# Routing of the second half of the tokens one head behind the first, two buffers of gates, gathers issued later

## The chip, the cores and the metric

The kernel runs on one core of a Trainium2 chip. The metric is the time of one execution on the device in microseconds (us), as the median of three runs. Engines: TensorE (PE) multiplies matrices, VectorE (DVE), ScalarE (ACT) and GpSimd (POOL) compute elementwise, and SyncE (SP) issues transfers between memory and the on-chip buffer. GpSimd issues the indirect transfers (gathers). Each engine takes its instructions strictly in the order in which they are written down for it.

## The reference

One layer of a decoder: two groups of attention heads, their output projection, and then PEER, a layer of 16,384 experts of one neuron each. The change is about PEER:

```
q = (xt @ w_query).reshape(T, PEER_HEADS, 2, PEER_HALF)
scores = jnp.einsum('thpc,hpnc->thpn', q, sub_keys)
vals, idx = lax.top_k(scores, PEER_TOPK)
cand = (vals[..., 0, :, None] + vals[..., 1, None, :]).reshape(T, PEER_HEADS, 256)
top_vals, top_c = lax.top_k(cand, PEER_TOPK)
experts = i1 * PEER_N_KEYS + i2       # i1, i2: the two key numbers of each chosen pair
gates = softmax(top_vals)
u = take(expert_down, experts);  hdn = gelu(einsum('ted,td->te', u, x))
y = einsum('te,ted->td', gates * hdn, take(expert_up, experts))
```

There are 512 tokens of width 2048, 8 heads, 128 keys for each half of a query, and 16 experts a head: 128 experts per token.

## The kernel before

All products are made with three matmuls in place of one (`mm3`, L96 to L101): an operand is split into `hi`, which ScalarE rounds, and `lo`, the rest, which GpSimd or VectorE subtracts (`load_split`, L94).

**Routing** (L523 to L616). `choose(hh, b0, queries)` handles one head for two blocks of 128 tokens. For each of the two half-queries it takes scores from PE (`sc`, L555) and finds the best 16 (`top16`: MAX8 at L532 and what follows); then it builds 50 candidates, finds the best 16 of them, and picks their numbers with a one-hot `oh` (L580 compares, L582 multiplies, on GpSimd for one block of two, L583 sums on VectorE). A first pass over 8 heads does blocks 2 and 3. Its `queries(hp)` multiplies with a slab of the query weights on PE (`pq`, two pieces of 24 matmuls of 128x512), for all four blocks at once, and keeps the queries of blocks 0 and 1 in `kept`. A second pass over 8 heads does blocks 0 and 1 from `kept`. `pq`, `sc` and other small products share the PSUM tag `aux` with four buffers.

**Two ways through the experts.** The first 320 tokens go through all experts densely: for each of 128 slabs of 128 experts, `down_tile` (48 matmuls `dn` of 128x320, the result in `hold`), multiplied by the gates (`gate_tile`), and then the up loop. The last 192 tokens take their 128 experts with 384 gathers (`gather_step`, L490 to L521): GpSimd fetches 128 rows (L507) into one of `NROW` = 4 buffers `rows`, and VectorE uses them (L510 for `down`, L518 for `up`), 64 and 64 for the first list (`e`), 128 and 128 for the second (`g`). A use is tied to a place in PE's order by a dependency that has no semaphore and only orders instructions (`PACE`).

**Gates** (L637 to L682): ten chunks of 32 tokens. VectorE makes one-hots `o2` and `o1` (L670, L671), ScalarE scales them, PE multiplies them (`gm`, L677), ScalarE copies into `stg` (L680), and each chunk is stored to `g_d` in memory. Each 8 tokens hold one `gather_step`, 40 in all.

**The expert loop**: 28 down tiles are stored to memory (`hid_d`) and read back late, 10 are held, with a gather step each; the scheduler puts many of these 38 into the order of the routing and the gates, where PE has room. Then 16 groups `g` of 16 steps `c`: an up step loads, splits (L793, L794) and multiplies 24 times (`up`), adds into `yacc` (L799 in the first group, L801 later), and every second step does one further down tile, or late in the loop, for the last 76 steps, reads a stored one back, and multiplies one `hold` by its gates (L775). The gates of four experts are one tile:

```
if e % 4 == 0:
    gt[0] = xp.tile([P, NGC, 4, GC], F32, tag="gt", name=f"gt{e}", bufs=1)
    DMA.dma_start(gt[0], g_d[:, :, e:e + 4, :].rearrange("c p e t -> p c e t"))
```

Gathers are paced by a counter in each up step, 1.6 a step as long as there are down tiles and 0.9 after:

```
due += 1.6 if e < NE1 - SPILL else 0.9
while due >= 1:
    gather_step(mm)
    due -= 1
```

Of the kernel before, what the change touches and what calls it, by code (L numbers as in the profile page):

```python
# [8 lines left out]
F32 = mybir.dt.float32  # L9
# [9 lines left out]
P = 128  # L19
S = 512  # L20
NB = S // P
D = 2048
# [7 lines left out]
PH = 8  # L30
TK = 16
HK = PH * TK
NE1 = 128
NEXP = NE1 * NE1
GC = 32
ND = 320
NDB = -(-ND // P)
NGC = ND // GC
NTC = S // GC
GB = NB - 1  # L40
NE = 64
EB = GB - 1
RB = 2
E0 = P - NE
ER = P // NE
# [14 lines left out]
def peer_block(ctx, tc, x, x_t, w_qk, w_v, w_fg, w_o, w_pq, sub_keys, down_t, down, up_t, up,  # L60
# [47 lines left out]
        G.tensor_tensor(r[:, :width], m[:, :width], mhalf[:, :width], ALU.pow)  # L108
        return r

    def diag_of(r, t, name):
        d = small.tile([P, P], F32, tag="diag", name=f"diag_{name}{t}", bufs=4)
        V.tensor_scalar(d, ident, r[:, t:t + 1], None, ALU.mult)
        return d

# [24 lines left out]
    with tc.tile_pool(name="xin", bufs=1, side="right") as xp:  # L140
        ones = xp.tile([P, P], F32, name="ones")
        G.memset(ones, 1.0)
        rps = bank("s", "rps")
        for t in range(NB):
            xx = xp.tile([P, D], F32, tag="x", name=f"x{t}", bufs=4)
            DMA.dma_start(xx, x[t * P:(t + 1) * P])
            junk = xp.tile([P, D], F32, name="junk", bufs=1)
            ss = xp.tile([P, 1], F32, name=f"ss{t}")
            A.activation(junk, xx, AF.Square, accum_out=ss)
            dg = diag_of(rstd_of(ss, D, f"x{t}", 1), 0, f"x{t}")  # L150
            PE.matmul(rps[:, t * P:(t + 1) * P], ones, dg, start=True, stop=True)
        xt = []
        for q in range(4):
            xx = xp.tile([P, 4, S], F32, name=f"xt{q}")
            DMA.dma_start(xx, x_t[:, q * 4:(q + 1) * 4])
            xt.append(xx)
            if q < 2:
                ahead.append(fetch(w_v[0, q], wts))
        rb = xp.tile([P, S], F32, name="rb")
        A.copy(rb, rps)  # L160
        ahead.append(load_split(None))
        ahead.insert(0, ahead.pop())
        for k in range(NK):
            xx = xt[k // 4][:, k % 4]
            (G if k % 2 else V).tensor_tensor(xx, xx, rb, ALU.mult)
            A.activation(xn[0][:, k], xx, AF.Copy, scale=gn[:, k:k + 1])
            V.scalar_tensor_tensor(xn[1][:, k], xx, gn[:, k:k + 1], xn[0][:, k].bitcast(F32), ALU.mult, ALU.subtract)
# [261 lines left out]
    for t in range(NB):  # L429
        V.tensor_reduce(hsum[:, t:t + 1], hss[:, t], AX.X, ALU.add)  # L430
        r = rstd_of(hsum[:, t:t + 1], D, f"h{t}", 1)
        hdiag.append(diag_of(r, 0, f"h{t}"))
        if t >= EB:
            rlast[t] = small.tile([P, 1], F32, name=f"rlast{t}")
            V.tensor_copy(rlast[t], r[:, 0:1])
# [28 lines left out]


    res = ctx.enter_context(tc.tile_pool(name="res2", bufs=1))
    top = res.tile([P, NB, PH, TK], F32, name="top")
    ex = res.tile([P, NB, PH, TK], F32, name="ex")
    gidx = res.tile([P, HK], I32, name="gidx")
    gidx_e = res.tile([P, EH], I32, name="gidx_e")  # L470
    gate_e = res.tile([P, EH], F32, name="gate_e")
# [9 lines left out]
        V.tensor_tensor(sel, sel, ident[:, r * NE:(r + 1) * NE], ALU.add)  # L481

    steps = [(w, part, j) for part, n in (("e", EH), ("g", HK)) for w in (down, up) for j in range(n)]
    lists = {"e": (gidx_e, gate_e), "g": (gidx, top.rearrange("p b h k -> p b (h k)")[:, GB])}
    dots = {p: ga.tile([P, n], F32, name=f"dots_{p}") for p, n in (("e", EH), ("g", HK))}
    coef = {p: ga.tile([P, n], F32, name=f"coef_{p}") for p, n in (("e", EH), ("g", HK))}
    yg = {}
    gstep = [0]

    def gather_step(after):  # L490

        n = gstep[0]
        gstep[0] += 1
        if n >= len(steps):
            return
        table, part, j = steps[n]
        ix, gate = lists[part]
        last = j == ix.shape[1] - 1
        if n == 0:
            hng["e"] = ga.tile([P, D], F32, tag="hy", name="hng_e")  # L500
            for r in range(ER):
                DMA.dma_start(hng["e"][r * NE:(r + 1) * NE], hn_d[:NE])
        elif part == "g" and steps[n - 1][1] == "e":
            hng["g"] = ga.tile([P, D], F32, tag="hy", name="hng_g")
            DMA.dma_start(hng["g"], hn_d[NE:])
        rows = ga.tile([P, D], F32, tag="rows", name=f"rows{n}", bufs=NROW)
        G.indirect_dma_start(out=rows, out_offset=None, in_=table,  # L507
                             in_offset=bass.IndirectOffsetOnAxis(ap=ix[:, j:j + 1], axis=0))
        if table is down:
            use = V.scalar_tensor_tensor(rows, rows, 1.0, hng[part], ALU.mult, ALU.mult, accum_out=dots[part][:, j:j + 1])  # L510
            if last:
                A.activation(coef[part], dots[part], AF.Gelu_apprx_tanh)
                V.tensor_tensor(coef[part], coef[part], gate, ALU.mult)
        elif j == 0:
            yg[part] = ga.tile([P, D], F32, tag="hy", name=f"yg_{part}")
            use = V.tensor_scalar(yg[part], rows, coef[part][:, j:j + 1], None, ALU.mult)
        else:
            use = V.scalar_tensor_tensor(yg[part], rows, coef[part][:, j:j + 1], yg[part], ALU.mult, ALU.add)  # L518
        tc.add_manual_dep(use.ins, after.ins.name, PACE, reason="pace")
        if table is up and last:  # L520
            fin_part(part)  # L521

    with tc.tile_pool(name="route", bufs=1, side="right") as rp:  # L523
# [84 lines left out]

        for hh in range(PH):
            choose(hh, NB - RB, queries)  # L610
        for dst, src in ((gidx_e, ex), (gate_e, top)):
            for r in range(ER):
                V.tensor_copy(dst[r * NE:(r + 1) * NE], src[E0:, EB].rearrange("p h k -> p (h k)")[:, r * EH:(r + 1) * EH])
        V.tensor_copy(gidx, ex[:, GB])
        for hh in range(PH):
            choose(hh, 0, lambda hp: kept[:, hp])  # L616
    if "ex" in dbg:
        DMA.dma_start(dbg["ex"], ex)
        DMA.dma_start(dbg["gate"], top)
# [18 lines left out]
    with tc.tile_pool(name="gates", bufs=1, side="right") as gp:  # L638
# [21 lines left out]
        for ch in range(NGC):  # L660
# [20 lines left out]
                gather_step(mm)  # L681
            DMA.dma_start(g_d[ch], stg)  # L682


    yp = ctx.enter_context(tc.tile_pool(name="yp", bufs=1, side="right"))
    yacc = yp.tile([P, NK, ND], F32, name="yacc")
    with tc.tile_pool(name="exp", bufs=1, side="right") as xp:
# [2 lines left out]
        fin = {}  # L690

        def fin_square(src, b, q):
            junk = xp.tile([P, S], F32, tag="gt", name="fjunk", bufs=1)
            n = src.shape[0]
            A.activation(junk[:n], src, AF.Square, accum_out=fss[b][:n, q:q + 1])

# [67 lines left out]
            gather_step(mm)  # L764
        pslot, npslot = 0, (NTC - NGC) * NK * GC // ND
        due = 0.0
        gt = [None]

        def gate_tile(e):

            if e % 4 == 0:
                gt[0] = xp.tile([P, NGC, 4, GC], F32, tag="gt", name=f"gt{e}", bufs=1)
                DMA.dma_start(gt[0], g_d[:, :, e:e + 4, :].rearrange("c p e t -> p c e t"))
            hv = hold[e].rearrange("p (c t) -> p c t", c=NGC)
            V.tensor_tensor(hv, hv, gt[0][:, :, e % 4, :], ALU.mult)  # L775

        for e in range(NG):
            gate_tile(e)
        for g in range(NE1 // NG):
# [8 lines left out]
            for c in range(NK):  # L788
                raw = xp.tile([P, NG, P], F32, tag="uraw", name="uraw", bufs=3)
                DMA.dma_start(raw, up_t[g, c])  # L790
                uh = xp.tile([P, NG, P], F32R, tag="uhi", name="uhi", bufs=2)
                ul = xp.tile([P, NG, P], F32R, tag="ulo", name="ulo", bufs=2)
                A.activation(uh, raw, AF.Copy)  # L793
                V.tensor_tensor(ul, raw, uh.bitcast(F32), ALU.subtract)  # L794
                ps = aux("up")
                for j in range(NG):
                    mm = mm3(ps[:, :ND], (uh[:, j], ul[:, j]), pp[j], j == 0, j == NG - 1)
                if g == 0:
                    V.tensor_copy(yacc[:, c], ps[:, :ND])  # L799
                else:  # L800
                    V.tensor_tensor(yacc[:, c], yacc[:, c], ps[:, :ND], ALU.add)  # L801
                e = HOLD + g * NG + c // 2
                if c % 2 and e < NE1:
                    if e < NE1 - SPILL:
                        down_tile(e, (V, V))
                    else:
                        hold[e] = hold_p.tile([P, ND], F32, tag="hold", name=f"hold{e}")
                        DMA.dma_start(hold[e], hid_d[e - (NE1 - SPILL)])
                if c % 2 and (g + 1) * NG + c // 2 < NE1:
                    gate_tile((g + 1) * NG + c // 2)  # L810
                due += 1.6 if e < NE1 - SPILL else 0.9
                while due >= 1:
                    gather_step(mm)
                    due -= 1
                if g == NE1 // NG - 1 and c == NK - 1:
                    assert gstep[0] >= len(steps)
                if g == NE1 // NG - 2 and c == 4:
                    fin_load()
                if g == NE1 // NG - 1 and c % 4 == 3:
                    fin_quarter(c // 4)  # L820
# [74 lines left out]
```

## Time and profile before

| | |
|---|---|
| median of three runs | 3359.06 us (3356.17 to 3362.79) |
| profiled execution | 3360.41 us |
| its span, first to last instruction | 3358.6 us |
| mean granted TensorE clock | 0.969 of full speed |
| PE, DVE, ACT, POOL busy | 3114.4, 2492.9, 1227.9, 968.4 us |
| moved by DMA | 846.50 MB |

The time is the execution's; all rows of the trace count from the span's first instruction. Busy times of engines overlap.

### The profile page before, as it was taken

To read this page: it belongs to the slowest core of one execution; us is meant where nothing else is said; L and a number is where in the kernel's file an instruction comes from. 1 tells how busy PE (TensorE), PEld (TensorE's weight loads), DVE (VectorE), ACT (ScalarE), POOL (GpSimd) and SP (SyncE) were. 2 spreads that over 40 slices of the span, in tenths; PEclk is the share of its full clock that TensorE was granted. 3 is DMA by queue.
4 is the path that set the end of the run, shared out by engine and by line. 5 is a ranking of instruction groups with operands and counts; after the bars stand their busy time and mean duration, and the time that the engine had idled before them with its cause. 6 is when DMAs were issued, how large, how long until landed. Compare 5 with 4: busy or idle time off the path is not lost.

```text
span 3358.6 us, 47197 instructions
## 1 busy us (share of the span) xinstructions
PE 3114.4 (93%) x18265; PEld 2845.3 (85%) x18265; DVE 2492.9 (74%) x3723; ACT 1227.9 (37%) x1875; POOL 968.4 (29%) x529
## 2 busy tenths in 40 slices
PE   6999999999999978888999999999889999998887
PEld 4887778878877767787999998999889999998887
DVE  5226664454356698997889998988788899988975
ACT  3224444342232235886333332333333333332233
POOL 2000000000024455665424433333333344432210
PEclk9999999999999978999999999999999999999999
DMA  4222222114332234988899999999899999999973
GB/s 180 96 95 75 68 67 78 65 61 138 129 132 82 100 134 138 340 325 330 318 382 392 393 371 371 386 360 369 332 353 367 363 400 399 369 390 360 365 291 119
DMA packets 215793, 846.50 MB, mean 252 GB/s; under 512 B 20945, under 2 KB 69457, under 8 KB 163217
## 3 DMA queue, kind: packets, MB, share of 16 engines
q1 hardware_dynamic: 159424, 439.37, 36.6%
q0 software_dynamic: 55296, 402.68, 30.1%
q8 instruction: 143, 2.34, 0.3%
q10 hardware_dynamic: 848, 1.44, 0.1%
q14 instruction: 82, 0.66, 0.1%
HBM read 806.31 MB, written 35.91 MB: 251 GB/s over the span
## 4 chain that ended last, share of the span: by engine, by line
PE 67%; DVE 13%; DMA 9%; issue 5%; POOL 3%; ACT 2%; ACTq 0%; SPq 0%; DVEq 0%; POOLq 0%
PE up L99 7%; PE up L101 6%; PE up L100 6%; PE dn L99 5%; PE dn L100 5%; PE dn L101 5%; DMA gt<-g_d 5%; PE mm L101 4%; PE mm L100 4%; PE mm L99 4%; DVE rows L510 3%; POOL lo L94 2%; DVE ulo L794 2%; DMA uraw<-in_up_t 2%; PE po L100 2%
## 5 line engine op out<-in xcount | busy, mean ns | idle before, releaser
L99 PE MATMUL up<-hn,ulo 128*128 128x320 f32 x2048 | 654.5, 320 | 87.5 <-DVE ulo L794 81.1
L99 PE MATMUL dn<-hn,lo 128*128 128x320 f32 x2048 | 657.1, 321 | 70.2 <-POOL lo L94 61.1
L93 ACT ACTIVATE hi<-raw 128x1024 fp32r<-128x1024 f32 x416 | 439.7, 1058 | 661.5 <-PE dn L101 206.7
L100 PE MATMUL dn<-hn,hi 128*128 128x320 f32 x2048 | 653.1, 319 | 0.0
L101 PE MATMUL dn<-hn,hi 128*128 128x320 f32 x2048 | 649.8, 317 | 0.0
L100 PE MATMUL up<-hn,uhi 128*128 128x320 f32 x2048 | 646.8, 316 | 0.9 <-DVE hn L786 0.9
L101 PE MATMUL up<-hn,uhi 128*128 128x320 f32 x2048 | 646.3, 316 | 0.0
L94 DVE TENSOR_TENSOR lo<-raw,hi 128x1024 fp32r<-128x1024 f32 x320 | 390.1, 1225 | 310.9 <-ACT hi L93 309.8
L793 ACT ACTIVATE uhi<-uraw 128x1024 fp32r<-128x1024 f32 x256 | 271.6, 1061 | 696.5 <-PE up L101 536.1
L99 PEld LDWEIGHTS up<-hn,ulo 128*128 128x128 f32 x2048 | 397.3, 194 | 104.4 <-DVE ulo L794 94.0
L99 PEld LDWEIGHTS dn<-hn,lo 128*128 128x128 f32 x2048 | 393.3, 192 | 80.9 <-POOL lo L94 70.4
L100 PEld LDWEIGHTS up<-hn,uhi 128*128 128x128 f32 x2048 | 397.5, 194 | 1.2 <-DVE hn L786 1.2
L101 PEld LDWEIGHTS up<-hn,uhi 128*128 128x128 f32 x2048 | 396.9, 194 | 0.0
L100 PEld LDWEIGHTS dn<-hn,hi 128*128 128x128 f32 x2048 | 393.7, 192 | 0.1
L101 PEld LDWEIGHTS dn<-hn,hi 128*128 128x128 f32 x2048 | 392.6, 192 | 0.0
L507 POOL DMA_INDIRECT rows<-in_up,gidx x128 | 222.9, 1741 | 388.7 <-DVE yg_g L518 365.8
L507 POOL DMA_INDIRECT rows<-in_down,gidx x128 | 207.3, 1620 | 425.6 <-DVE rows L510 394.5
L794 DVE TENSOR_TENSOR ulo<-uraw,uhi 128x1024 fp32r<-128x1024 f32 x256 | 311.1, 1231 | 21.6 <-ACT uhi L793 20.9
L94 POOL TENSOR_TENSOR lo<-raw,hi 128x1024 fp32r<-128x1024 f32 x96 | 250.0, 2606 | 197.7 <-ACT hi L93 197.4
L518 DVE SCALAR_TENSOR_TENSOR yg_g<-rows,coef_g,yg_g 128x2048 f32<-128x2048 f32 x127 | 298.0, 2347 | 0.0
L510 DVE SCALAR_TENSOR_TENSOR rows<-rows,hng_g 128x2048 f32<-128x2048 f32 x128 | 290.8, 2286 | 4.5 <-DMA hng_g<-hn_d 4.3
L99 PE MATMUL mm<-xn,lo 128*128 128x512 f32 x512 | 204.4, 399 | 0.0
(258 smaller groups left out, 4989.4 us busy)
## 6 DMA issues: line engine op xcount, KB each, us to landing
raw<-in_down_t SPq DMA_DIRECT2D x256, 512.0 KB
uraw<-in_up_t SPq DMA_DIRECT2D x256, 512.0 KB
raw<-in_w_qk SPq DMA_DIRECT2D x64, 512.0 KB
g_d<-stg SPq DMA_DIRECT2D x10, 2048.0 KB
gt<-g_d SPq DMA_DIRECT2D x32, 640.0 KB
raw<-in_w_v SPq DMA_DIRECT2D x32, 512.0 KB
raw<-in_w_o SPq DMA_DIRECT2D x32, 512.0 KB
raw<-in_w_pq SPq DMA_DIRECT2D x32, 512.0 KB
```

The source lines that it names most:

```text
L93: A.activation(hi, raw, AF.Copy)
L94: (lo_on or V).tensor_tensor(lo, raw, hi.bitcast(F32), ALU.subtract)
L99: PE.matmul(ps, a[1], b[0], start=first, stop=False)
L100: PE.matmul(ps, a[0], b[1], start=False, stop=False)
L101: return PE.matmul(ps, a[0], b[0], start=False, stop=last)
L507: G.indirect_dma_start(out=rows, out_offset=None, in_=table, in_offset=bass.IndirectOffsetOnAxis(ap=ix[:, j:j + 1], axis=0))
L510: use = V.scalar_tensor_tensor(rows, rows, 1.0, hng[part], ALU.mult, ALU.mult, accum_out=dots[part][:, j:j + 1])
L518: use = V.scalar_tensor_tensor(yg[part], rows, coef[part][:, j:j + 1], yg[part], ALU.mult, ALU.add)
L793: A.activation(uh, raw, AF.Copy)
L794: V.tensor_tensor(ul, raw, uh.bitcast(F32), ALU.subtract)
```

## The change

1. The second pass of `choose` runs one head behind the first: after head `hh` of blocks 2 and 3 comes head `hh - 1` of blocks 0 and 1. The copies of the gathers' numbers and gates are placed after the last head of the first pass; the gates of the last block get a tile of their own, `gate_g`.
2. The tiles of gates `gt` have two buffers, and each is loaded one tile ahead.
3. The issue of a gather is tied to the place in PE's order of the use three steps back (`marks`).
4. The late pace is 0.8 in place of 0.9.
5. `top` and `ex` lie in a pool that ends after the gates, and the small `diag` tiles in pools that end earlier, which makes the memory for the second `gt`.

```diff
     res = ctx.enter_context(tc.tile_pool(name="res2", bufs=1))
-    top = res.tile([P, NB, PH, TK], F32, name="top")
-    ex = res.tile([P, NB, PH, TK], F32, name="ex")
+    rt_cm = tc.tile_pool(name="routes", bufs=1, side="right")
+    rtp = rt_cm.__enter__()
+    top = rtp.tile([P, NB, PH, TK], F32, name="top")
+    ex = rtp.tile([P, NB, PH, TK], F32, name="ex")
+    gate_g = res.tile([P, HK], F32, name="gate_g")
...
         rows = ga.tile([P, D], F32, tag="rows", name=f"rows{n}", bufs=NROW)
-        G.indirect_dma_start(out=rows, out_offset=None, in_=table,
+        ld = G.indirect_dma_start(out=rows, out_offset=None, in_=table,
                              in_offset=bass.IndirectOffsetOnAxis(ap=ix[:, j:j + 1], axis=0))
+        marks.append(after.ins.name)
+        if n >= NROW:
+            tc.add_manual_dep(ld.ins, marks[n - NROW + 1], PACE, reason="pace")
...
         for hh in range(PH):
             choose(hh, NB - RB, queries)
-        for dst, src in ((gidx_e, ex), (gate_e, top)):
-            for r in range(ER):
-                V.tensor_copy(dst[r * NE:(r + 1) * NE], src[E0:, EB].rearrange("p h k -> p (h k)")[:, r * EH:(r + 1) * EH])
-        V.tensor_copy(gidx, ex[:, GB])
-        for hh in range(PH):
-            choose(hh, 0, lambda hp: kept[:, hp])
+            if hh == PH - 1:
+                for dst, src in ((gidx_e, ex), (gate_e, top)):
+                    for r in range(ER):
+                        V.tensor_copy(dst[r * NE:(r + 1) * NE], src[E0:, EB].rearrange("p h k -> p (h k)")[:, r * EH:(r + 1) * EH])
+                V.tensor_copy(gidx, ex[:, GB])
+                V.tensor_copy(gate_g, top[:, GB].rearrange("p h k -> p (h k)"))
+            if hh:
+                choose(hh - 1, 0, lambda hp: kept[:, hp])
+        choose(PH - 1, 0, lambda hp: kept[:, hp])
...
-        gt = [None]
+        gt = []
 
         def gate_tile(e):
 
             if e % 4 == 0:
-                gt[0] = xp.tile([P, NGC, 4, GC], F32, tag="gt", name=f"gt{e}", bufs=1)
-                DMA.dma_start(gt[0], g_d[:, :, e:e + 4, :].rearrange("c p e t -> p c e t"))
+                while len(gt) < 2 and e + 4 * len(gt) < NE1:
+                    e1 = e + 4 * len(gt)
+                    gt.append(xp.tile([P, NGC, 4, GC], F32, tag="gt", name=f"gt{e1}", bufs=2))
+                    DMA.dma_start(gt[-1], g_d[:, :, e1:e1 + 4, :].rearrange("c p e t -> p c e t"))
             hv = hold[e].rearrange("p (c t) -> p c t", c=NGC)
             V.tensor_tensor(hv, hv, gt[0][:, :, e % 4, :], ALU.mult)
+            if e % 4 == 3:
+                gt.pop(0)
...
-                due += 1.6 if e < NE1 - SPILL else 0.9
+                due += 1.6 if e < NE1 - SPILL else 0.8
```

What this does to the order of the engines is seen at three places. On PE in the routing, between the second half-query of a head and the first of the next (`qt` is the first pass's query, `kept` the second pass's), before:

```order
L101 MATMUL pq_7275<-hn_6788,hi 128x512
L555 MATMUL sc_7339<-sk,qt 128x128 x2
L99 MATMUL pq_7401<-hn_6788,lo 128x512
L100 MATMUL pq_7401<-hn_6789,hi 128x512
L101 MATMUL pq_7401<-hn_6788,hi 128x512
```

and in the changed order:

```order
L101 MATMUL pq_7279<-hn_6788,hi 128x512
L562 MATMUL sc_7343<-sk,qt 128x128 x2
L562 MATMUL sc_7405<-sk,kept 128x128 x2
L562 MATMUL sc_7424<-sk,kept 128x128 x2
L99 MATMUL pq_7482<-hn_6788,lo 128x512
L100 MATMUL pq_7482<-hn_6789,hi 128x512
L101 MATMUL pq_7482<-hn_6788,hi 128x512
```

The scores of the second pass now stand between the queries of two heads; before, they stood after the queries of all 8. Beside them stood down tiles: the first transposition of the stage of gates had 600 `dn` matmuls (12.5 tiles) ahead of it and has 168 (3.5 tiles) now, the gates themselves hold 744 and now 714, and the stretch behind them, up to the first pair of up steps, some 10 tiles and now 942 matmuls (19.6 tiles).

On GpSimd from the end of the gates to the held tiles (`lo` of down tiles and gathers of the first list), before:

```order
L507 DMA rows_10313<-in_down,gidx_e 128x2048
L94 TENSOR_TENSOR lo<-raw,hi 128x1024
L507 DMA rows_10340<-in_down,gidx_e 128x2048
L94 TENSOR_TENSOR lo<-raw,hi 128x1024
L507 DMA rows_10369<-in_down,gidx_e 128x2048
```

and in the changed order:

```order
L511 DMA rows_10401<-in_down,gidx_e 128x2048
L511 DMA rows_10428<-in_down,gidx_e 128x2048
L94 TENSOR_TENSOR lo<-raw,hi 128x1024
L511 DMA rows_10455<-in_down,gidx_e 128x2048
L511 DMA rows_12328<-in_down,gidx_e 128x2048
L94 TENSOR_TENSOR lo<-raw,hi 128x1024 x2
L511 DMA rows_12394<-in_down,gidx_e 128x2048
L511 DMA rows_12460<-in_down,gidx_e 128x2048
L94 TENSOR_TENSOR lo<-raw,hi 128x1024 x20
L511 DMA rows_12526<-in_down,gidx_e 128x2048
```

Gathers and `lo` alternated; now two gathers stand between one or two `lo`, and behind the gates 20 `lo` stand in a row without a gather.

On SyncE at the first loads of gates (`g_d` the stores of the gates, `gt` their loads), before:

```order
L682 DMA g_d<-stg 128x4096
L82 DMA raw<-in_down_t 128x1024 x3
L773 DMA gt_12919<-g_d 128x10x128
L82 DMA raw<-in_down_t 128x1024
L790 DMA uraw<-in_up_t 128x1024 x2
```

and in the changed order:

```order
L692 DMA g_d<-stg 128x4096
L773 DMA hid_d<-hold_11686 128x320
L82 DMA raw<-in_down_t 128x1024 x3
L773 DMA hid_d<-hold_11750 128x320
L787 DMA gt_12925<-g_d 128x10x128
L82 DMA raw<-in_down_t 128x1024
L787 DMA gt_12927<-g_d 128x10x128
L82 DMA raw<-in_down_t 128x1024
L773 DMA hid_d<-hold_11814 128x320
```

Two tiles of gates are loaded at once instead of one, with stored down tiles still behind them.

## Rows read from the trace of the kernel before

**Rows 1.** The page's busy time of each engine over the span.

```profile
PE 3114.4 (93%) x18265; PEld 2845.3 (85%) x18265; DVE 2492.9 (74%) x3723; ACT 1227.9 (37%) x1875; POOL 968.4 (29%) x529
```

**Rows 2.** Busy by stretch: length, engines (instructions), PE clock, DMA share, GB/s.

```profile
950.00:1152.00 202.00, 192.91 (x826) 150.15 (x825) 112.22 (x528) 42.57 (x69) 90.72 (x39) 0.99 0.28 96
1152.00:1316.00 164.00, 122.98 (x692) 115.85 (x691) 148.73 (x651) 55.48 (x71) 87.52 (x38) 0.82 0.36 125
1316.00:1560.00 244.00, 204.85 (x1380) 194.72 (x1380) 233.59 (x158) 202.62 (x444) 157.14 (x69) 0.94 0.84 314
...
1652.00:2000.00 348.00, 343.65 (x2307) 342.58 (x2306) 322.00 (x283) 117.95 (x144) 136.77 (x75) 0.99 0.99 383
2000.00:2634.00 634.00, 588.00 (x3835) 581.37 (x3835) 538.90 (x586) 200.01 (x249) 209.78 (x131) 0.96 0.95 363
2634.00:2981.00 347.00, 342.79 (x2310) 341.99 (x2309) 324.48 (x273) 118.83 (x146) 151.65 (x77) 1.00 0.98 385
2981.00:3215.00 234.00, 203.38 (x1246) 194.55 (x1245) 205.19 (x196) 62.49 (x76) 66.00 (x48) 0.93 0.98 366
```

**Rows 3.** The same view for 100 us within a good stretch.

```profile
2700.00:2800.00 100.00, 99.89 (x678) 99.62 (x677) 95.39 (x79) 34.87 (x43) 47.01 (x23) 1.00 1.01 396
```

**Rows 4.** Uses of `down` rows, second list: min/median/max ns, first to last start.

```profile
L510 DVE SCALAR_TENSOR_TENSOR rows<-rows,hng_g x128: 2283/2286/2294, 2017.1 to 2636.8; 128x2048 f32<-128x2048 f32 x128
```

**Rows 5.** Waits in 2000 to 2634: us in total, times, longest.

```profile
DVE hold L775 <- DMA gt<-g_d: 48.9, 9, 10.0
...
PE up L99 <- DVE ulo L794: 39.8, 10, 7.4
```

**Rows 6.** Timeline of DVE near 2361: start, us, instruction, the wait before it.

```profile
2361.19 0.49 DVE L775 TENSOR_TENSOR hold<-hold,gt 128x320 f32<-128x320 f32 x1 [8.21 <-DMA gt<-g_d]
2361.60 1.22 DVE L94 TENSOR_TENSOR lo<-raw,hi 128x1024 fp32r<-128x1024 f32 x1
```

**Rows 7.** Lines in 950 to 1152: busy, mean ns | idle before, releaser.

```profile
L583 DVE TENSOR_REDUCE ex<-oh 128x16 f32<-128x800 f32 x14 | 13.8, 987 | 11.7 <-POOL oh L582 11.5
...
L555 PE MATMUL sc<-sk,qt 128*128 128x128 f32 x60 | 10.7, 300 | 9.1 <-ACT qt L604 6.5 <-DMA sk<-in_sub_keys 2.6
...
L532 DVE MAX8 vv<-sc 128x8 f32<-128x128 f32 x30 | 8.6, 288 | 70.9 <-PE sc L555 70.9
```

**Rows 8.** Lines in 1152 to 1316.

```profile
L583 DVE TENSOR_REDUCE ex<-oh 128x16 f32<-128x800 f32 x18 | 17.3, 973 | 12.2 <-POOL oh L582 12.2
```

**Rows 9.** Single lines as in rows 4; idle before L532.

```profile
L532 DVE MAX8 vv<-sc x64: 273/280/302, 964.8 to 1292.8; 128x8 f32<-128x128 f32 x64
...
  PE sc L555: 79.2, 9
...
L648 DVE CAST stg<-ex x1: 359/359/359, 1306.8 to 1306.8; 128x384 int32<-128x384 f32 x1
...
L680 ACT COPY stg<-gm x80: 1018/1096/1220, 1318.5 to 1558.6; 128x512 f32<-128x512 f32 x80
...
L799 DVE COPY yacc<-up x16: 482/487/495, 1651.6 to 1759.2; 128x320 f32<-128x320 f32 x16
```

**Rows 10.** Lines of DVE in 2700 to 2800.

```profile
L518 DVE SCALAR_TENSOR_TENSOR yg_g<-rows,coef_g,yg_g 128x2048 f32<-128x2048 f32 x23 | 54.0, 2347 | 0.0
L794 DVE TENSOR_TENSOR ulo<-uraw,uhi 128x1024 fp32r<-128x1024 f32 x14 | 16.9, 1220 | 0.0
...
L801 DVE TENSOR_TENSOR yacc<-yacc,up 128x320 f32<-128x320 f32 x14 | 6.8, 483 | 1.4 <-PE up L101 1.3
L786 DVE TENSOR_TENSOR hn<-hold,hn 128x320 fp32r<-128x320 f32 x8 | 3.5, 487 | 0.0
```

**Rows 11.** Waits of DVE from 3004 to the end.

```profile
DVE hold L775 <- DMA gt<-g_d: 4.4, 3, 4.0
```

**Rows 12.** Lines in 1316 to 1560.

```profile
L99 PE MATMUL dn<-hn,lo 128*128 128x320 f32 x247 | 85.7, 347 | 34.4 <-POOL lo L94 34.4
...
L507 POOL DMA_INDIRECT rows<-in_down,gidx_e x39 | 69.2, 1773 | 48.4 <-DVE rows L510 38.4 <-PE gm L677 6.8 <-issue 1.4
```

More of the change, by code (lines that the diff above doesn't have):

```diff
@@ L109, in rstd_of, with diag_of @@
         return r
-    def diag_of(r, t, name):
-        d = small.tile([P, P], F32, tag="diag", name=f"diag_{name}{t}", bufs=4)
+    def diag_of(r, t, name, pool):
+        d = pool.tile([P, P], F32, tag="diag", name=f"diag_{name}{t}", bufs=4)
         V.tensor_scalar(d, ident, r[:, t:t + 1], None, ALU.mult)
@@ L149, in peer_block @@
             A.activation(junk, xx, AF.Square, accum_out=ss)
-            dg = diag_of(rstd_of(ss, D, f"x{t}", 1), 0, f"x{t}")
+            dg = diag_of(rstd_of(ss, D, f"x{t}", 1), 0, f"x{t}", xp)
             PE.matmul(rps[:, t * P:(t + 1) * P], ones, dg, start=True, stop=True)
@@ L431, in peer_block @@
         r = rstd_of(hsum[:, t:t + 1], D, f"h{t}", 1)
-        hdiag.append(diag_of(r, 0, f"h{t}"))
+        hdiag.append(diag_of(r, 0, f"h{t}", hpool))
         if t >= EB:
@@ L483, in peer_block @@
     steps = [(w, part, j) for part, n in (("e", EH), ("g", HK)) for w in (down, up) for j in range(n)]
-    lists = {"e": (gidx_e, gate_e), "g": (gidx, top.rearrange("p b h k -> p b (h k)")[:, GB])}
+    lists = {"e": (gidx_e, gate_e), "g": (gidx, gate_g)}
     dots = {p: ga.tile([P, n], F32, name=f"dots_{p}") for p, n in (("e", EH), ("g", HK))}
@@ L488, in peer_block @@
     gstep = [0]
+    marks = []
     def gather_step(after):
@@ L682, in peer_block @@
             DMA.dma_start(g_d[ch], stg)
+    rt_cm.__exit__(None, None, None)
     yp = ctx.enter_context(tc.tile_pool(name="yp", bufs=1, side="right"))
@@ L692, in fin_square @@
         def fin_square(src, b, q):
-            junk = xp.tile([P, S], F32, tag="gt", name="fjunk", bufs=1)
+            junk = xp.tile([P, S], F32, tag="gt", name="fjunk", bufs=2)
             n = src.shape[0]
```

## The prediction

> **What bounds the kernel now.** TensorE (PE) is busy in 93% of the span of 3358.6 us [rows 1], in triples of matmuls that the change leaves alone. So the question is not what PE does but where it does nothing. I cut the span at the starts of the groups of `yacc` additions and read the busy time stage by stage [rows 2]. A stretch in which nothing disturbs PE gives the price of a matmul: 678 in 100 us, 0.1475 us each [rows 3]. A down tile is 48 of them, 7.08 us; a step of the up loop is 24, 3.54 us. Length less count times 0.1475 is what PE lost in a stretch of [rows 2]: 7.7 us in 1652 to 2000, **68.3** in 2000 to 2634, 6.3 in 2634 to 2981, **50.2** in 2981 to 3215. The two poor ones are the stretch in which the gathers of `down` rows for the last 128 tokens run, with up and down tiles (their use at L510 lies between 2017 and 2637 [rows 4]), and the stretch after the down tiles have ended.
>
> Next, the waits in 2000 to 2634 [rows 5]: VectorE (DVE) waits 48.9 us, 9 times, for the load of a tile of gates, and PE waits 39.8 us for DVE's `ulo`. The timeline shows that these are one thing [rows 6]: at 2361 the multiplication of `hold` by `gt` stands at the head of DVE's queue and waits 8.21 us, with a `lo` right behind it, and every `ulo` further back is late for PE. `gt` has one buffer, so its load can only be issued when the fourth multiplication of the tile before is done.
>
> Before 1652 DVE bounds. In routing it waits 79.2 us for scores [rows 9], nearly all in the first pass, and 11.5 and 12.2 in the two passes for GpSimd's `oh` [rows 7, 8]; in the stage of gates, 1316 to 1560, it is busy in 233.6 of 244 us [rows 2].
>
> **1. Routing.** The first MAX8 starts at 964.8 and the first cast of the stage of gates at 1306.8 [rows 9]: 342 us. Less the 79.2 us of waits for scores, 263 us are work and GpSimd waits, 16.4 for each of 16 calls of `choose`; the change removes none of it. Of the 79.2 us, 70.9 fall into the first 7.5 heads (30 of 32 MAX8s on `sc`) [rows 7], 9.5 a head. With the second pass one head behind, DVE has 16.4 us more to do per head. The queries of a head cost PE two groups of 48 matmuls; 766 of those and 60 small ones fill 192.9 us [rows 2, 7], so about 12 us a group and 24 a head, against 33 us of DVE per head. DVE should wait for the first head and part of the second only; I leave 19 us of waits. 263 and 19 are 282: the gates start at 1247, 60 us earlier. Between 1237 (9.5 us of waits, the first head's alone) and 1343 (the rival below) is possible.
>
> But the second pass covered something. Today PE does 12.5 down tiles before the stage of gates, mostly beside it; in the changed order there are 3.5. The stage of gates keeps about 15 (14.9 for 15.5) and, bound by DVE, its 252 us (1306.8 to the last copy of L680 at 1558.6 [rows 9]), so it ends at 1499; then 19.6 tiles follow in place of 10, 139 us, before the first up step, 3.5, and some 4 for the loads of gates: first `yacc` copy near 1645, against 1651.6 [rows 9]. **Worth 7 us**, out of 62: the rest has only moved. Bounds: with no waits left but the first head's and all tiles at full rate, 25; with routing as in the rival, minus 89.
>
> **2. Two buffers of gates.** Each load is now issued a whole tile ahead: eight up steps, which with their four down tiles take 57 us of PE. The waits of [rows 5] go, and the DVE work behind them is on time. At the rate of its neighbours the stretch would lose about 12 instead of 68.3 us, a gain of 57. I don't take all of it, for the next resource is near: the DMA engines moved 363 GB/s in 634 us, 230 MB; at the 385 of 2634 to 2981 this takes 598 us, at the 396 of the best 100 us 581 [rows 2, 3]. I take **43**, between 36 and 53. The bounds are 0 (something else is late at once) and 57. DVE has room: 539 us of work in 591 is 91%, against 95.4 in 100 us [rows 3]. Loading ahead adds no bytes. In the two neighbours 14 us are lost, in part to the same loads: **4**. A copy to `gate_g` and one more set of small pools are one DVE instruction of well under a microsecond, hidden in the waits of the second head.
>
> **3. The pace at the end.** From the last stored tile on, an up step pays `ulo` 1.22, `yacc` 0.48, half a `hold` and half a `hn` of 0.49 each, and 0.9 of a gather's 2.35 [rows 6, 10]: 4.30 us of DVE against 3.54 of PE, so DVE bounds it. At 0.8 it is 4.07. 384 gathers less 40 beside the gates, 10 beside the held tiles and 1.6 in each of 180 up steps leave 46 for the last 76 steps: 51 steps at 4.30 and 25 at 3.54 are 308 us; 57.5 at 4.07 and 18.5 at 3.54 are 299.5. Gain 8.5, and 4.4 of gate waits there [rows 11]; half of the rest of the 50.2 may be other things: **14**, bounds 0 and 35.
>
> **4. The gather's issue.** GpSimd now issues a gather behind the use three steps back. In the up loop its order holds little but gathers, so a gather that is issued one place later is still some three uses ahead: 0. In the stage of gates GpSimd today stands with a gather at its head for 38.4 us (waiting for the row buffer that DVE holds), with a `lo` behind it, and PE waits 34.4 us for `lo` [rows 12]. The new order puts `lo` in front. PE gains there, but DVE bounds the stage: I take **0**, bounds 0 and 7; up to 34 would come through only if the tiles behind the gates became fewer, and the order shows 19.6.
>
> **Sum:** 7 + 43 + 4 + 14 = 68. The profiled execution took 3360.4 us, its span 3358.6; the median of three runs is 1.3 below the execution. 3360.4 less 68 is 3292.4, on the median's footing 3291.
>
> **Rivals.** *DMA bounds the middle.* For it: the share of DMA is 0.95 to 1.01 from 1652 to 3215 [rows 2, 3]. Then removing the stall removes little: the stretch gets 10 us shorter, the end 8, and routing nothing: about 3340. Against it: 385 and 396 GB/s are measured beside 363, and in that stretch DVE's waits fall on one line. The Trainium skill (DMA: Bandwidth & Descriptors, Specifications) gives about 358 GB/s from memory per core, and its section Bandwidth says that a core that streams alone gets more, up to 425. By 358 the 230 MB would take 643 us and the buffers be worth nothing; the trace has 385 over 347 us [rows 2], more than that, and the measurement decides.
>
> *Everything comes through:* 57 in the middle, 10 beside it, 35 at the end, 25 in routing: 127, about 3232. For it: PE's granted clock was 0.93 and 0.96 in the poor stretches and 0.99 and 1.00 in the good ones [rows 2], so that stalls may cost twice.
>
> *Slower: routing alternates.* PE runs in order, and now scores of the second pass stand before the next head's queries. `aux` has four buffers for queries and scores of both passes; a group of queries takes one that DVE must have read, and its `lo` stands on GpSimd behind an `oh` that DVE must first have made. If one of the two groups of a head thus stays uncovered, routing takes 8 times 12, 96 us, more: gates at 1343, first `yacc` at 1741, and with 61 gained later about 3387. It decides from 75 us on (gates after 1322, over 9 us of new waits a head). For it: GpSimd and `oh` already make DVE wait 24 us [rows 7, 8]. Against it: 24 us of PE fit into 33 of DVE, and one group has a whole call of `choose` to hide in.
>
> *No change:* the part of gates and routing loses some 60 (fewer tiles, a slower clock beside small matmuls: 0.82 in 1152 to 1316 [rows 2]) and gives back what the rest gains: 3355.
>
> **How the numbers follow.** Forecast 0.50 (3260 to 3315), DMA 0.18, everything 0.13, no change 0.09, routing 0.10. The range, 3218 to 3350, leaves out routing, no change and a tail of "everything". About 0.2% (6.7 us) is what a measurement of this kernel can tell from none: faster 0.80, same 0.09, slower 0.11.
>
> **What the profile after should show.** The first cast of the gates near 1247 and the last L680 copy near 1499; the first `yacc` copy within 15 us of 1645. Hardly any wait of `hold` for `gt`, against 53 us in [rows 5, 11]; the stretch of `down` gathers at about 591 us, with a DMA rate of 385 to 396 GB/s and PE at a clock near 0.99; after the last down tile some 14 us less. Wrong would be: `vv` waiting for `sc` more than 90 us in routing; the waits for `gt` gone and PE losing as much to another load; the up steps at the end still at 4.3 us.

## The result and the profile after

The changed kernel takes 3315.23 us (median of four runs, 3313.15 to 3325.38) against 3359.57 (four runs): a ratio of 0.9874, 95% interval 0.9852 to 0.9897. The forecast was faster, 3291, between 3218 and 3350. The gain of 44 us is two thirds of the 68 that were forecast, and all of it comes from one of the four parts, the buffers of gates. One run of a later kernel, the one with one buffer of gates, took 6014 us and is in no ratio.

The busy time by stretch, cut as in [rows 2] at the same places of the program (length, PE, PEld, DVE, ACT, POOL, PE clock, DMA share, GB/s):

```profile
950.00:1250.00 300.00, 243.99 (x1056) 196.48 (x1054) 242.41 (x1167) 57.61 (x95) 126.64 (x56) 0.90 0.27 90
1250.00:1505.00 255.00, 210.51 (x1396) 198.06 (x1397) 252.80 (x172) 208.15 (x449) 166.56 (x72) 0.94 0.82 307
1505.00:1660.00 155.00, 150.20 (x974) 144.31 (x973) 65.56 (x56) 55.52 (x73) 79.58 (x40) 1.00 0.78 269
1660.00:2000.00 340.00, 338.70 (x2292) 337.90 (x2291) 318.92 (x280) 117.28 (x144) 134.79 (x74) 1.00 1.00 390
2000.00:2592.00 592.00, 580.26 (x3864) 575.40 (x3863) 543.98 (x588) 202.14 (x250) 212.88 (x131) 0.99 0.99 388
2592.00:2930.00 338.00, 335.51 (x2263) 334.98 (x2262) 317.71 (x267) 116.23 (x142) 146.40 (x77) 0.99 1.00 393
2930.00:3170.00 240.00, 208.43 (x1315) 200.26 (x1314) 206.05 (x205) 66.09 (x80) 64.31 (x43) 0.94 0.95 353
```

The places that the forecast named, in the changed kernel's views of single lines, as in [rows 4, 9]; the line behind the MAX8s is DVE's idle time before them:

```profile
L539 DVE MAX8 vv<-sc x64: 271/280/301, 966.9 to 1242.3; 128x8 f32<-128x128 f32 x64
...
  PE sc L562: 35.2, 9
...
L658 DVE CAST stg<-ex x1: 359/359/359, 1255.6 to 1255.6; 128x384 int32<-128x384 f32 x1
...
L690 ACT COPY stg<-gm x80: 1030/1092/1244, 1267.9 to 1504.1; 128x512 f32<-128x512 f32 x80
...
L815 DVE COPY yacc<-up x16: 484/486/494, 1659.8 to 1761.2; 128x320 f32<-128x320 f32 x16
...
L817 DVE TENSOR_TENSOR yacc<-yacc,up x240: 472/483/489, 1771.8 to 3294.9; 128x320 f32<-128x320 f32 x120
```

Before, the last addition into `yacc` started at 3342.1. The starts of the first `yacc` addition of a group give the ledger (us):

| from | to | before | after | difference | forecast |
|---|---|---|---|---|---|
| first MAX8 | first cast of the gates | 342.0 | 288.7 | -53.3 | -60 |
| there | last copy of the gates | 251.8 | 248.5 | -3.3 | 0 |
| there | first `yacc` copy | 93.0 | 155.7 | +62.7 | +54 |
| there | group 3 | 348.2 | 340.3 | -7.9 | -4, with the row after next |
| there | group 8 (the `down` gathers) | 634.4 | 590.0 | -44.4 | -43 |
| there | group 11 | 346.5 | 344.8 | -1.7 | |
| there | last addition | 361.4 | 360.0 | -1.4 | -14 |

With 2 us later at the first MAX8 these are the 47.2 us between the spans of the two profiles, 3358.6 and 3311.4. The first three rows together are a loss: 686.9 us from the first MAX8 to the first `yacc` copy have become 692.8.

Of the 35.2 us of waits for scores, 10.6 lie before the first MAX8, so outside of the first row of the ledger. The first four waits of the changed kernel's DVE (start, us, instruction, the wait before it), and the first of the kernel before:

```profile
966.91 0.30 DVE L539 MAX8 vv<-sc 128x8 f32<-128x128 f32 x1 [10.60 <-PE sc L562]
980.72 0.30 DVE L539 MAX8 vv<-sc 128x8 f32<-128x128 f32 x1 [10.85 <-PE sc L562]
1005.80 0.30 DVE L539 MAX8 vv<-sc 128x8 f32<-128x128 f32 x1 [8.26 <-PE sc L562]
1039.42 0.30 DVE L539 MAX8 vv<-sc 128x8 f32<-128x128 f32 x1 [0.80 <-PE sc L562]
```

```profile
964.78 0.30 DVE L532 MAX8 vv<-sc 128x8 f32<-128x128 f32 x1 [10.07 <-PE sc L555]
```

The five that follow are between 0.45 and 1.31 us long. So from the first MAX8 to the first cast DVE waited 69.1 us for scores before and 24.6 after.

What went away is seen in the waits. Over the whole execution of the kernel before, DVE waited for tiles of gates 22 times (us in total, times, longest):

```profile
DVE hold L775 <- DMA gt<-g_d: 81.5, 22, 10.0
```

The changed kernel has no such row. In the stretch of the `down` gathers, as in [rows 5], the multiplication now waits for ScalarE's result alone, never longer than 1.1 us, and PE's wait for `ulo` is down from 39.8 to 9.5:

```profile
DVE hold L789 <- ACT hold L643: 15.3, 24, 1.1
...
PE up L99 <- DVE ulo L810: 9.5, 6, 2.8
```

By the price of [rows 3] PE still loses 592 less 3864 times 0.1475, 22 us, in this stretch. Half of it is the hand-over from the first list of gathers to the second, the first 126 us:

```profile
2000.00:2126.00 126.00, 120.95 (x779) 117.39 (x778) 114.14 (x127) 43.40 (x58) 47.79 (x29) 0.97 0.99 387
```

### The profile page after: what moved, and what is told of

Its sections match the earlier page's. It is cut to its first block, busy times and chain, and to the rows that moved or that the text cites. A ratio compares the mean times of both kernels' runs of the same rounds, so it can differ in the third digit from the quotient of the medians.

```text
span 3311.4 us, 47208 instructions
## 1 busy us (share of the span) xinstructions
PE 3098.8 (94%) x18265; PEld 2828.8 (85%) x18265; DVE 2497.5 (75%) x3724; ACT 1214.8 (37%) x1863; POOL 967.6 (29%) x529
## 4 chain that ended last, share of the span: by engine, by line
PE 42%; DVE 11%; issue 5%; DMA 3%; POOL 2%; ACT 0%; SPq 0%; ACTq 0%; DVEq 0%; POOLq 0%
PE up L99 7%; PE up L100 7%; PE up L101 7%; PE dn L99 7%; PE dn L100 7%; PE dn L101 6%; DVE o L680 2%; DMA uraw<-in_up_t 2%; DVE o L681 2%; DVE rows L517 2%; DVE ulo L810 1%; DVE yg_g L525 1%; POOL rows L511 1%; POOL lo L94 1%; DVE hn L802 1%
## 5 line engine op out<-in xcount | busy, mean ns | idle before, releaser
L99 PE MATMUL up<-hn,ulo 128*128 128x320 f32 x2048 | 646.6, 316 | 55.6 <-DVE ulo L810 55.1
L99 PE MATMUL dn<-hn,lo 128*128 128x320 f32 x2048 | 650.3, 318 | 44.3 <-POOL lo L94 41.8
L100 PE MATMUL up<-hn,uhi 128*128 128x320 f32 x2048 | 640.3, 313 | 0.9 <-DVE hn L802 0.9
L101 PE MATMUL up<-hn,uhi 128*128 128x320 f32 x2048 | 639.6, 312 | 0.0
L100 PEld LDWEIGHTS up<-hn,uhi 128*128 128x128 f32 x2048 | 391.2, 191 | 1.2 <-DVE hn L802 1.2
L101 PEld LDWEIGHTS up<-hn,uhi 128*128 128x128 f32 x2048 | 390.9, 191 | 0.0
L100 PEld LDWEIGHTS dn<-hn,hi 128*128 128x128 f32 x2048 | 389.2, 190 | 0.0
L101 PEld LDWEIGHTS dn<-hn,hi 128*128 128x128 f32 x2048 | 388.8, 190 | 0.0
```

The costliest lines, as they stand in the source:

```text
L99: PE.matmul(ps, a[1], b[0], start=first, stop=False)
L100: PE.matmul(ps, a[0], b[1], start=False, stop=False)
L101: return PE.matmul(ps, a[0], b[0], start=False, stop=last)
```

## The experiments

Twelve kernels ran, each against the kernel before on its own chip. For each the ratio with its 95% interval stands first; a median from another chip moves by some us, so positions in the traces are compared as lengths, from the first MAX8 on.

**One buffer of gates.**

```diff
-                while len(gt) < 2 and e + 4 * len(gt) < NE1:
-                    e1 = e + 4 * len(gt)
-                    gt.append(xp.tile([P, NGC, 4, GC], F32, tag="gt", name=f"gt{e1}", bufs=2))
-                    DMA.dma_start(gt[-1], g_d[:, :, e1:e1 + 4, :].rearrange("c p e t -> p c e t"))
+                gt.append(xp.tile([P, NGC, 4, GC], F32, tag="gt", name=f"gt{e}", bufs=1))
+                DMA.dma_start(gt[-1], g_d[:, :, e:e + 4, :].rearrange("c p e t -> p c e t"))
```

> The changed kernel with one buffer of gates, loaded when it is needed, as before; everything else as changed. If the removed waits for gates are the gain, the three stretches of the up loop up to the last down tile get back the 54 us that they lost (7.9, 44.4 and 1.7), while the 8 us lost before the first yacc copy stay: about 3367 us, slower than the kernel before. If the gain came from the later issue of the gathers or from the order of routing, it stays between 3315 and 3325.

Measured: 1.0005 (0.9985 to 1.0024), 3362.25 us. The whole gain is gone. From the first `yacc` copy to the start of group 11 it takes 1329.3 us, the kernel before 1329.0, the changed one 1275.2, and DVE waits for tiles of gates again, 87.7 us in 18 waits. That it would be slower than the kernel before can't be told from this.

**The buffers alone.** The kernel before, with the buffers and the pools that make room for them (the edits of the issue, the routing and the pace undone).

> The kernel before with two buffers of gates alone (and the move of small tiles that makes room for them): old order of routing, no dependency on the gathers' issue, pace 0.9. If the buffers are the whole gain, within 6 us of 3314. If routing, issue and pace only looked worthless one at a time and carry something together, above 3325.

Measured: 0.9845 (0.982 to 0.987), 3307.07 us. The buffers alone are worth all that the change is worth: the interval overlaps that of the changed kernel (0.9852 to 0.9897) and its centre lies 0.3% lower. The lengths say where: 682.0 us from the first MAX8 to the first `yacc` copy, against 692.8, and 1275.8 from there to group 11, against 1275.2. The kernel before took 686.9 us for the first of these, so the buffers seem to save some 5 us there too.

**The old order of routing, the rest as changed.**

```diff
         for hh in range(PH):
             choose(hh, NB - RB, queries)
...
-            if hh:
-                choose(hh - 1, 0, lambda hp: kept[:, hp])
-        choose(PH - 1, 0, lambda hp: kept[:, hp])
...
+        for hh in range(PH):
+            choose(hh, 0, lambda hp: kept[:, hp])
```

> The changed kernel with the second pass behind the whole first pass, as before. Theory: the down tiles that covered the second pass are done behind the gates instead, and routing gave nothing back: the first yacc copy at about 1652 instead of 1660, the time about 3307 us. Rival, my forecast: the new order is worth 7 us, so about 3322.

Measured: 0.9871 (0.9845 to 0.9897), 3313.9 us: no difference that can be told. Its gates start 52 us later after the first MAX8 (340.6 us for 288.7), and its first `yacc` copy comes 690.6 us after the first MAX8, against 692.8. It lies in the middle between the two numbers that were expected, so the time speaks for neither; the lengths show that 52 us of earlier gates bring nothing.

**No dependency on the gathers' issue, the rest as changed.**

```diff
-        if n >= NROW:
-            tc.add_manual_dep(ld.ins, marks[n - NROW + 1], PACE, reason="pace")
```

> The changed kernel without the dependency that ties a gather's issue to the use three steps back. Theory: in the up loop GpSimd has little but gathers, and DVE bounds the gates, so the time stays within 5 us of 3315. Rival: the later issue keeps the lo of the down tiles from standing behind a gather that waits, and PE loses beside the gates what it waited there before, up to 34 us: up to 3349.

Measured: 0.9888 (0.9861 to 0.9915), 3320.64 us: 5 us above the changed kernel, not to be told apart from it by the intervals. The first `yacc` copy comes 698.1 us after the first MAX8, 5 us later. How far a single profile can be trusted here is seen from two kernels below that are the changed one up to this place: with the pace 0.9 it takes 695.6 us, with the last 46 gathers left out 695.8. So 2 to 5 us are left, not clear of the spread of 3.

**Both undone, pace 0.8.** The old routing and no dependency, which differs from the run with old routing only by the dependency, and from the buffers alone only by the pace.

> Two buffers of gates, old routing, no dependency on the gathers' issue, pace 0.8: the run with old routing less the dependency, or the buffers alone with the lower pace. In the old order the dependency left 13.4 down tiles beside the gates instead of 15.5, and the first yacc copy came at 1660 instead of 1650.5; so without it about 9 us less than the run with old routing, 3303 to 3309, and the pace moves the buffers alone (3307) by less than 4. Rival: the difference between those two runs is the pace, then 3313.

Measured: 0.9854 (0.9832 to 0.9875), 3306.66 us, not to be told from the buffers alone. The first `yacc` copy comes after 681.9 us, against 690.6 with the dependency. So in the old order the dependency costs 8.7 us up to there, clear of the 1 us between the three kernels without it (681.9, 682.0 and 682.9); in the new order it gives 2 to 5 or nothing. Seen the other way, the new order of routing costs 2 to 5 us up to there with the dependency (690.6 to between 692.8 and 695.8) and 16 without it (682 to 698.1). What differs in the old order can be read beside the gates; first with the dependency (the run with old routing), in 1310 to 1557 (lines, with what they waited for):

```profile
L94 POOL TENSOR_TENSOR lo<-raw,hi 128x1024 fp32r<-128x1024 f32 x28 | 96.4, 3463 | 38.9 <-ACT hi L93 38.9
L99 PE MATMUL dn<-hn,lo 128*128 128x320 f32 x216 | 79.1, 366 | 36.7 <-POOL lo L94 36.7
L511 POOL DMA_INDIRECT rows<-in_down,gidx_e x39 | 76.5, 1961 | 34.0 <-PE dn L99 18.5 <-DVE rows L517 8.1 <-issue 3.5
```

and in the buffers alone, 1309 to 1562:

```profile
L94 POOL TENSOR_TENSOR lo<-raw,hi 128x1024 fp32r<-128x1024 f32 x32 | 93.0, 2906 | 42.6 <-ACT hi L93 42.4
L99 PE MATMUL dn<-hn,lo 128*128 128x320 f32 x249 | 87.1, 350 | 34.3 <-POOL lo L94 34.3
L511 POOL DMA_INDIRECT rows<-in_down,gidx_e x39 | 69.2, 1775 | 48.4 <-DVE rows L515 36.8 <-PE gm L683 8.5 <-issue 1.2
```

The gather no longer waits 36.8 us for DVE's row buffer, but PE's wait for `lo` is the same 34 to 37 us, and 28 `lo` fit beside the gates instead of 32, each 3.46 us long instead of 2.91: two tiles more are left for the stretch behind. In the new order PE's wait for `lo` did fall, from 31.6 us without the dependency to 19.0 in the changed kernel, beside the gates from 1256 to 1505:

```profile
L99 PE MATMUL dn<-hn,lo 128*128 128x320 f32 x241 | 83.3, 346 | 19.0 <-POOL lo L94 19.0
```

**Eight tiles written into the routing** (`EARLY` is 1).

```diff
             choose(hh, NB - RB, queries)
+            for e in range(NE1 - SPILL + hh * EARLY, NE1 - SPILL + (hh + 1) * EARLY):
+                down_tile(e, (G, G))
+                DMA.dma_start(hid_d[e - (NE1 - SPILL)], hold[e])
...
-        for e in range(NE1 - SPILL, NE1):
+        for e in range(NE1 - SPILL + PH * EARLY, NE1):
```

> The changed kernel with one of the stored down tiles written behind the scores of each head of the first pass, so that 8 tiles stand in the routing's order, where PE was idle for 56 of 300 us. Theory: the earlier gates were worth nothing because the down tiles that used to fill PE's idle time beside the second pass moved behind the gates; with 8 tiles of 7.08 us back in idle time the first yacc copy comes 35 to 55 us earlier and the time is 3265 to 3285. Rival: PE's idle time there is needed (a tile makes the next head's queries late for DVE), gates start 40 us later, and the time stays at 3310 to 3320.

Measured: 0.985 (0.9825 to 0.9875), 3310.95 us, no better than the changed kernel. The rival held. Routing takes 335.7 us instead of 288.7; DVE's idle time before the MAX8s is

```profile
  PE sc L577: 68.6, 10
```

against 35.2 in the changed kernel, which is 33 of the 47 us, and the first `yacc` copy comes after 688.9 us.

**Eight tiles left out.** The down tiles of 8 of the 28 stored slabs are not computed, and others are read back in their place.

```diff
-        for e in range(NE1 - SPILL, NE1):
+        for e in range(NE1 - SPILL + 8, NE1):
             down_tile(e, (G, G))
...
-                        DMA.dma_start(hold[e], hid_d[e - (NE1 - SPILL)])
+                        DMA.dma_start(hold[e], hid_d[max(8, e - (NE1 - SPILL))])
```

> The changed kernel with 8 of the 28 stored down tiles left out (the reload takes a stored tile in their place, so their experts' values are not computed); routing as changed. Theory: in the new order the stretch behind the gates is PE's work alone, and each tile there is 7.08 us on the path: first yacc copy near 1603, the time 57 us less, about 3258. Rival: the gates or their loads set the start of the up loop, and less than 25 us are gained.

Measured: 0.9696 (0.9674 to 0.9718), 3252.96 us, 60 less than the changed kernel by the ratios. From the first MAX8 to the first `yacc` copy it takes 632.5 us, 60.3 less than in the changed kernel; 8 tiles at 7.08 us are 56.6. All of it is taken from the stretch behind the gates (96.3 us for 155.7):

```profile
1505.00:1607.00 102.00, 98.37 (x631) 94.83 (x631) 68.28 (x60) 39.74 (x55) 46.81 (x25) 0.98 0.94 333
```

**The pace 0.9, the rest as changed.**

```diff
-                due += 1.6 if e < NE1 - SPILL else 0.8
+                due += 1.6 if e < NE1 - SPILL else 0.9
```

> The changed kernel with 0.9 gathers a step in the last 76 steps in place of 0.8. Theory: that stretch is bound by the bytes it has to move until the last gather, which the pace doesn't change, so within 4 us of 3315. Rival, my forecast: DVE bounds a step there and the lower pace gives 8.5 us, so about 3324.

Measured: 0.9869 (0.9843 to 0.9895), 3314.9 us. The pace is worth nothing: from group 11 to the last addition it takes 358.6 us at 0.9 and 359.9 at 0.8. The old order gives the same answer: 362.5 in the buffers alone, at 0.9, and 362.3 with both undone, at 0.8.

**Two gathers beside each held tile, and this with the tiles in the routing.**

```diff
             mm = down_tile(e, (G, V))
             gather_step(mm)
+            gather_step(mm)
```

> The changed kernel with two gather steps beside each of the 10 held tiles instead of one, so that 10 of the 46 gathers leave the last 76 steps for the stretch behind the gates, where the share of DMA was 0.78. If bytes bound the last steps until the last gather, each gather of 1 MB costs some 2.7 us there: 20 to 27 us less, 3288 to 3295. If not, within 5 us of 3315.

> Both the tiles in the routing and the second gather beside each held tile. If the two theories hold and don't share a resource, the gains add: 3240 to 3265. If the gathers then lie in the way of what is left behind the gates, no better than the tiles alone, 3265 to 3285.

Measured: 0.9923 (0.9898 to 0.9947), 3331.69 us, and 0.9917 (0.9894 to 0.9939), 3331.25: both slower than the changed kernel, and outside of all that was expected. The last part does get shorter, 354.8 us for 359.9 from group 11, but by 5 us and not by 27; with the tiles in the routing it takes 351.3. Even the 5 are not clear: in the kernels here that keep all 46 gathers in the last 76 steps this part takes between 353.7 us (one buffer of gates) and 370.0 (tiles in the routing). And 18.6 us are lost before: from the first `yacc` copy to group 11 it takes 1293.8 us for 1275.2. The first group takes 125.3 us for 112.0, and the hand-over between the lists, a group earlier there, makes its group 134.4 us long, for 125.9. In the first group PE has one long wait, for a `ulo` that stands on DVE, which does five uses of gathered rows in a row before it (1668.9 to 1687.5, with 3.5 us of waits for rows):

```profile
PE up L99 <- DVE ulo L811: 7.6, 1, 7.6
```

The other 6 of its 13 us were not taken apart. In the hand-over, 1905 to 2040, DVE waits for the first rows and for the tokens' values of the second list, and PE for a `lo` behind them:

```profile
PE dn L99 <- DVE lo L94: 9.4, 2, 7.9
DVE rows L517 <- DMA rows<-in_down,gidx: 7.9, 3, 2.9
DVE rows L517 <- DMA hng_g<-hn_d: 5.2, 1, 5.2
```

**The reloads spread out**, on top of the kernel with both undone.

```diff
-                        DMA.dma_start(hold[e], hid_d[e - (NE1 - SPILL)])
+                        ld = DMA.dma_start(hold[e], hid_d[e - (NE1 - SPILL)])
+                        tc.add_manual_dep(ld.ins, mm.ins.name, PACE, reason="pace")
```

> The same with each reload of a stored tile tied to the up step that it belongs to, so that SyncE issues them one by one between the loads of up weights and not five to eight in a row. Theory: what was left of the loss in the last 76 steps are the starts of groups (steps of 10 to 12 us), where SyncE stands behind a reload that waits for its buffer, up weights come late and DVE waits for the reload: 10 to 25 us less than the run beside it, 3282 to 3297. Rival: the bursts of splitting at a group's start make these steps long, and nothing changes (within 5 us).

Measured: 0.9879 (0.986 to 0.9898), 3313.69 us: not better, and rather worse than its base of 3306.66, on the same chip. The last part takes 363.4 us for 362.3, and DVE's waits for reloads there were not less, 18.8 us for 15.2. My theory of the groups' starts fell.

**The last 46 gathers left out.** The sum over the gathered experts of the last 128 tokens stops 46 terms short.

```diff
-    steps = [(w, part, j) for part, n in (("e", EH), ("g", HK)) for w in (down, up) for j in range(n)]
+    steps = [(w, part, j) for part, n in (("e", EH), ("g", HK)) for w in (down, up) for j in range(n)][:-46]
...
-        last = j == ix.shape[1] - 1
+        last = j == ix.shape[1] - 1 or n == len(steps) - 1
```

> The changed kernel without the last 46 gathers of up rows (the sum over the gathered experts of the last 128 tokens stops there), all of which stand in the last 76 steps; the rest as changed. These steps took 335.5 us from the last down matmul to the last yacc addition, against 269 for PE alone. If the gathers (their bytes and their use on DVE) make these steps long, some 55 us go and the time is 3255 to 3270. If the splitting and the reloads at a group's start make them long, less than 25 us go, 3290 or more.

Measured: 0.9705 (0.9684 to 0.9725), 3256.48 us, 57 less than the changed kernel by the ratios, and the last part is 59 us shorter (300.9 us for 359.9). PE then runs at its full rate, 1429 matmuls in 210 us, 0.147 each; first the stretch of this kernel, then that of the changed one:

```profile
2960.00:3170.00 210.00, 209.87 (x1429) 209.35 (x1428) 126.59 (x185) 78.31 (x100) 0.75 (x1) 1.00 0.64 202
```

```profile
2960.00:3214.00 254.00, 221.25 (x1394) 211.69 (x1394) 215.34 (x214) 69.42 (x82) 59.40 (x43) 0.95 0.94 347
```

So each of these gathers costs 59 / 46, 1.28 us of the end on average; at the pace 0.9 it is 358.6 less 300.9 over 46, 1.25.

## Why the prediction was right, and where not

**Two buffers of gates: right.** 43 and 4 were forecast, 44.4 and 9.6 measured, and the run with one buffer gives all of it back. The buffers alone gave some 5 us more, ahead of the first `yacc` copy, where DVE had waited 8.2 us for tiles of gates; the forecast had left 4 there as lost. The rival "DMA bounds the middle" is refuted: the stretch of the `down` gathers ran at 388 GB/s, between the 385 and 396 from which the size was taken, and the share of DMA was 0.99. PE still loses 22 us in the stretch: half in the hand-over between the lists, which was not taken apart. The Trainium skill's 358 GB/s per core (DMA: Bandwidth & Descriptors, Specifications) is exceeded for 1270 us on end, as its section Bandwidth allows for a core that streams alone.

**Routing: the mechanism was right, the sign of a small difference wrong.** The step that was mis-sized is "worth 7 us": it measured a loss of 6 (692.8 us for 686.9), and of 11 for routing and dependency together against the buffers alone (682.0), the fairer measure. The gates started 53 us earlier instead of 60. The waits in this were forecast well: "the first head and part of the second only; I leave 19". The two waits at 980.72 and 1005.80 are 19.1 us, and the six after them add 5.5. The rest, "263 us are work and GpSimd waits", came out by luck. 10.1 of the 79.2 us of [rows 9] lie before the first MAX8, so the kernel before had 273 us besides its waits for scores, and the changed one has 264; 2 of the 9 are waits for `oh` (21.4 us for 23.7), the others were not taken apart. PE itself stood at three places in the routing of the changed kernel:

```profile
PE sc L562 <- ACT qt L611: 19.6, 15, 5.5
PE dn L99 <- POOL lo L94: 18.2, 4, 11.9
PE pq L99 <- DVE ii L542: 16.3, 6, 3.9
```

The larger miss is the stretch behind the gates, 155.7 us where I had 146.5: PE ran 974 matmuls in the 155 us from 1505, which at 0.1475 are 144. Of the other 11 the forecast had 4; where the rest went is open. That the earlier gates would be paid back by the tiles behind them is shown: without eight of those tiles the first `yacc` copy comes 60 us earlier, and with the old order of routing it comes at nearly the same place. The tiles have to run somewhere beside DVE's work, and the run with tiles in the routing shows that there was no free place: what PE gained, the next head's scores lost. The rival "routing alternates" had the right places, PE's waits for DVE (16.3 us, of the queries) and for `lo` (18.2, of down tiles), and too large a price: from the third head on DVE's new waits are some 1 us a head, not the nine from which it decides.

**The pace: wrong.** The step that failed is the one that adds up DVE's work, "4.30 us of DVE against 3.54 of PE, so DVE bounds it. At 0.8 it is 4.07". The steps with gathers took 4.6 us before (235.6 us from the last down matmul, 3005.1, to the last use at 3240.7, for 51 steps) and 4.4 after (254.6 for 57.5), so the sign that was named for being wrong, "the up steps at the end still at 4.3 us", came. DVE alone did not bound them, for it was busy in 204 of 236 us before and in 215 of 254 after. The stretch of the kernel before:

```profile
3005.00:3241.00 236.00, 204.54 (x1245) 194.40 (x1245) 204.09 (x198) 63.51 (x76) 59.99 (x43) 0.93 0.96 359
```

The sum of durations was itself too large, because DVE's instructions overlap by some 0.08 us in the trace (in [rows 6] one of 0.49 us starts at 2361.19 and the next at 2361.60): 4.30 us a step are 4.0 of busy time. What counts there is the number of gathers, not their pace: 1.28 us for each, as the run without them shows. A lower pace only spreads the same cost over more steps. What in a gather costs this much, its megabyte or its place in DVE's order, is not settled: ten fewer gave 5 us and not 13, within the spread of this part, and spreading the reloads gave none.

**The gather's issue: right in size, for this order.** 0 was forecast, and the time can't tell the run without it from the change. That "DVE bounds the stage" held (248.5 us of gates, 251.2 without). But what it does depends on the routing, which the prediction did not see: behind the old order it adds 8.7 us up to the first `yacc` copy, behind the new one it takes off 2 to 5 or nothing.

**The sum** was 68; 47 of it for the buffers came as 54, and the other 21 came as a loss of 7 (5.9 in routing, less 1.4 at the end, and 2 before the first MAX8). That the time fell into the range is owed to the buffers, which came out above their term, and to the width of the range. No kernel that does the whole work beats the buffers alone, 0.9845; 0.9854 with the lower pace and 0.985 with tiles in the routing can't be told from it.

## What to carry to other kernels

A wait that stands in the order of an engine with little slack costs the work behind it too; here 81.5 us of DVE's waiting for the loads of one kind of tile cost 54 us of the execution from the first `yacc` copy on, and one more buffer was the whole gain. Moving DVE's work to where DVE idles was worth nothing here, because PE's work that lay beside it had no other place: count both engines' idle time up to the point where they meet before giving a price. And a rate at which work is fed in changes nothing if its amount is what the stretch pays for: leave the work out once, and its average price is known. And read a wait by its place: a total over a stretch can hold one that lies before the stretch begins.

## What the runs showed that was not expected

The time of `lo` on GpSimd is not a constant: 128x1024 took 2.91 us on average beside the gates in the kernel with the buffers alone and 3.46 in the same stage with the gathers issued later, where the gathers' own instructions took 1.96 us instead of 1.78. What it met there was not tried.
